# Block sums of the feed-forward weights by adding transfers instead of GpSimd, other shares for VectorE, and a few steps in another order

## The chip, the core and the metric

The kernel runs on one core of a Trainium2 chip, as one launch. The metric is the device time of a launch in microseconds (us). The engines are TensorE (PE; PEld is its weight load), VectorE (DVE), ScalarE (ACT), GpSimd (POOL) and SyncE (SP, which here only issues transfers). A smaller number is better.

## What is computed

One step of a two-layer network over 640 tokens (512 latent ones, 128 of context) of width 1024. Each layer is a feed-forward half, a token mixer and a second feed-forward half. Each of the six is modulated by a shift, a scale and a gate, which are a matrix product of a conditioning vector, and is followed by a residual and a LayerNorm:

```python
def _ffn_half(x, mod, slot, w1, w3, w2, g, b):
    h = _modulate(x, mod[:, 3 * slot], mod[:, 3 * slot + 1])
    f = (jax.nn.silu(h @ w1) * (h @ w3)) @ w2
    return _residual_post_norm(x, f, mod[:, 3 * slot + 2], FFN_RES, g, b)
# mod = (silu(cond) @ w_mod + b_mod).reshape(9, 1024), once for the latent and once for the context tokens
# x <- LN(alpha * x + weight * gate * f)
```

All is fp32. The inner width of a feed-forward half is 2816, that is 22 blocks of 128 columns (j = 0 to 21).

## The kernel before

**Precision.** TensorE multiplies in a reduced form, so each operand is split into a high part (ScalarE copies it, L299, tiles `wh`) and a low part (the difference, L306, tiles `wl`), and each product is made of three matmuls (high x high, high x low, low x high).

**Columns of a feed-forward half.** The blocks j = 0, 1, 2 are multiplied in the plain way. Blocks 3 to 21 are `Pair`s (19 in each half, 76 in all): W1 and W3 of a block are taken together as a 2 x 2 matrix of blocks a11, a12, a21, a22 (each 128 x 512 in memory, 256 KB), the activations as another (b11 and so on, and combinations of them, tiles `ta`, `tb`, made once for each half), and the product is made of 7 block products instead of 8. For that the weights have to be combined: s1 = a21 + a22, s2 = s1 - a11, s3 = a11 - a21, s4 = a12 - s2. The 7 products are of 12 matmuls of 320 columns each, 84 in a pair. `Pair.run` gives their order; its small closures (`u3`, `c12`, `gate1`, ...) put the results together on VectorE and ScalarE and are called one product later, by `slot`.

**Chunks.** The 22 blocks go in chunks of 4 (one of them a pair), 3, 3, 4, 4 and 4. After each chunk come the 8 blocks of W2 (tiles `o`), whose results are added to x (`resid`, L610).

**Weights.** `Stream` loads and converts all weights in the order of their use. `load` issues a load from SP into one of two buffers of 512 KB. `get` converts as far ahead as six slots of `wh` and `wl` allow, so five blocks ahead of the one that TensorE takes. `combine` makes s1 to s4 of a pair on GpSimd (L259, four instructions) into four buffers `ws` of 256 KB. The low parts of s2 and s4 (`ON_POOL`) are made on GpSimd as well, the five others on VectorE.

**Modulation units.** A unit is 128 columns of the modulation, with 512 KB of weights; there are 144. The first 24 are made by TensorE at the beginning. The 120 others are shared out in `vecq` order: some on VectorE inside feed-forward halves (`vec_mods`: per unit 4 multiplications with a sum, L460, and one small step, L463, paced by a credit at each call of `mods`, three in a pair and one for each block of W2), 16 in each of the first three halves; the rest inside the two mixers on TensorE (`mod_beside`: 16 small matmuls, L397, and a step of two, L415), 40 in layer 0 and 32 in layer 1.

**Mixer and norm.** The mixer's order is a table written out by hand (`SCHEDULES`), the same in both kernels. `rows_norm` ends each of the six parts: it adds the last blocks to x, takes the statistics and makes the next modulated input; `coef` makes the norm coefficients of the next part (tiles `gam`, `bet`) from the modulation.

## Time and profile before

| | us |
|---|---|
| median of 3 runs | 2677.38 (2677.23 to 2682.13) |
| the profiled execution | 2677.22 |
| its span, first to last instruction | 2675.0 |
| TensorE busy | 2537.6 (95%) |
| VectorE busy | 2068.8 (77%) |
| GpSimd busy | 1243.9 (46%) |
| ScalarE busy | 1176.7 (44%) |

A share of the span is an average over parts with different limits. Matmuls overlap one another, so a busy TensorE can still be one that waits a little before each group; for that the same work is compared in several places.

### The profile page before, as it was taken

To read this page: it belongs to the slowest core of one execution; us is meant where nothing else is said; L and a number is where in the kernel's file an instruction comes from. 1 tells how busy PE (TensorE), PEld (TensorE's weight loads), DVE (VectorE), ACT (ScalarE), POOL (GpSimd) and SP (SyncE) were. 2 spreads that over 40 slices of the span, in tenths; PEclk is the share of its full clock that TensorE was granted. 3 is DMA by queue.
4 is the path that set the end of the run, shared out by engine and by line. 5 is a ranking of instruction groups with operands and counts; after the bars stand their busy time and mean duration, and the time that the engine had idled before them with its cause. 6 is when DMAs were issued, how large, how long until landed. Compare 5 with 4: busy or idle time off the path is not lost. (4 is left out here: it accounts for less than half of the span.)

```text
span 2675.0 us, 49819 instructions
## 1 busy us (share of the span) xinstructions
PE 2537.6 (95%) x18662; PEld 2437.0 (91%) x18662; DVE 2068.8 (77%) x3759; ACT 1176.7 (44%) x2596; POOL 1243.9 (46%) x973
## 2 busy tenths in 40 slices
PE   7999999899999999999989999998998999999997
PEld 6999999889778999999989999998996798999997
DVE  6589899856764879988987998898586558777776
ACT  5233333555574533333453333334555735334333
POOL 1345445522444555544565454454234456435554
PEclk9999999999999999999999999998999999999998
DMA  7333332355344233333223333323452331222222
GB/s 266 120 94 107 100 103 91 106 165 148 96 125 156 72 99 99 102 109 104 71 82 99 100 103 109 105 87 125 141 159 80 104 123 44 78 85 84 83 79 72
DMA packets 130544, 285.88 MB, mean 107 GB/s; under 512 B 16832, under 2 KB 34560, under 8 KB 129664
## 3 DMA queue, kind: packets, MB, share of 16 engines
q1 hardware_dynamic: 110720, 247.04, 29.3%
q10 hardware_dynamic: 19584, 35.66, 4.2%
q8 instruction: 148, 2.42, 0.4%
q14 instruction: 92, 0.75, 0.1%
HBM read 254.95 MB, written 8.81 MB: 99 GB/s over the span
## 5 line engine op out<-in xcount | busy, mean ns | idle before, releaser
L306 DVE TENSOR_TENSOR wl<-wr,wh 128x512 fp32r<-128x512 f32 (+1 forms) x524 | 510.0, 987 | 74.2 <-ACT wh L299 73.1
L299 ACT CAST wh<-wr 128x512 fp32r<-128x512 f32 (+1 forms) x570 | 332.7, 607 | 484.5 <-DMA wr<-in_w 309.2
L485 PE MATMUL o<-gh,wh 128*128 128x256 f32 (+1 forms) x1408 | 439.7, 312 | 19.7 <-ACT gh L886 12.1
L485 PE MATMUL o<-gl,wh 128*128 128x256 f32 (+1 forms) x1408 | 438.6, 312 | 1.8
L485 PE MATMUL o<-gh,wl 128*128 128x256 f32 (+1 forms) x1408 | 436.4, 310 | 0.0
L847 PE MATMUL p<-hh,wh 128*128 128x320 f32 x1216 | 377.1, 310 | 10.9 <-DVE pm L858 10.8
L847 PE MATMUL p<-hl,wh 128*128 128x320 f32 x1216 | 377.2, 310 | 6.6 <-DVE hl L1010 6.6
L847 PE MATMUL p<-hh,wl 128*128 128x320 f32 x1216 | 377.4, 310 | 0.7 <-DVE wl L306 0.7
L259 POOL TENSOR_TENSOR ws<-wr 128x512 f32<-128x512 f32 x76 | 110.4, 1453 | 544.8 <-DMA wr<-in_w 508.5
L299 ACT CAST wh<-ws 128x512 fp32r<-128x512 f32 x304 | 185.7, 621 | 355.1 <-PE p L847 128.4
L306 POOL TENSOR_TENSOR wl<-ws,wh 128x512 fp32r<-128x512 f32 x152 | 239.9, 1582 | 189.2 <-ACT wh L299 188.6
L610 DVE SCALAR_TENSOR_TENSOR x<-o,gat,x 128x128 f32<-128x128 f32 (+2 forms) x404 | 193.0, 525 | 137.1 <-PE o L485 135.5
L485 PEld LDWEIGHTS o<-gh,wh 128*128 128x128 f32 x1408 | 267.7, 190 | 23.4 <-ACT gh L886 15.0
L485 PEld LDWEIGHTS o<-gl,wh 128*128 128x128 f32 x1408 | 267.9, 190 | 6.8 <-DVE gl L891 4.8
L485 PEld LDWEIGHTS o<-gh,wl 128*128 128x128 f32 x1408 | 267.5, 190 | 0.0
L847 PEld LDWEIGHTS p<-hh,wh 128*128 128x128 f32 x1216 | 228.9, 188 | 13.2 <-issue 12.2
L847 PEld LDWEIGHTS p<-hl,wh 128*128 128x128 f32 x1216 | 229.1, 188 | 7.7 <-DVE hl L1010 7.7
L847 PEld LDWEIGHTS p<-hh,wl 128*128 128x128 f32 x1216 | 229.2, 189 | 1.8 <-DVE wl L306 1.5
L460 DVE SCALAR_TENSOR_TENSOR scr<-wv,cb 128x512 f32<-128x512 f32 x192 | 174.8, 910 | 0.0
L259 POOL TENSOR_TENSOR ws<-wr,wr 128x512 f32<-128x512 f32 x76 | 130.4, 1715 | 0.6 <-DVE wl L306 0.6
L259 POOL TENSOR_TENSOR ws<-wr,ws 128x512 f32<-128x512 f32 x76 | 130.4, 1716 | 0.0
L306 DVE TENSOR_TENSOR wl<-ws,wh 128x512 fp32r<-128x512 f32 x152 | 129.2, 863 | 0.0
(434 smaller groups left out, 6604.3 us busy)
## 6 DMA issues: line engine op xcount, KB each, us to landing
wr<-in_w SPq DMA_DIRECT2D x176, 512.0 KB, 4.2
wm<-in_wmod ACTq DMA_DIRECT2D x136, 256.0 KB, 3.1
wr<-in_w SPq DMA_DIRECT2D x128, 256.0 KB, 2.7
wv<-in_wmt SPq DMA_DIRECT2D x96, 256.0 KB, 4.1
wm<-in_wmod SPq DMA_DIRECT2D x56, 256.0 KB, 5.3
wr<-in_w SPq DMA_DIRECT2D x64, 192.0 KB, 2.4
wr<-in_wint SPq DMA_DIRECT2D x24, 512.0 KB, 4.3
wr<-in_wo SPq DMA_DIRECT2D x16, 512.0 KB, 3.8
```

Source lines behind the costliest of these rows:

```text
L259: G.tensor_tensor(out=o, in0=x0, in1=x1, op=op)
L299: S.copy(hl[0], src[:, c0:c1])
L306: eng.tensor_tensor(out=t2, in0=src, in1=t.bitcast(F32), op=ALU.subtract)
L460: V.scalar_tensor_tensor(out=scr, in0=w[2 * i + hf], scalar=1.0, in1=cb[:, 2 * st + hf, :], op0=ALU.mult, op1=ALU.mult, accum_out=a[:, 2 * ...
L485: PE.matmul(out[:, :cn], whl[a][:, k, :], b[:, c0:c0 + cn], start=k == 0 and i == 0, stop=k == n - 1 and i == 2)
L610: V.scalar_tensor_tensor(out=c, in0=src, scalar=gat[:, d, s:s + 1], in1=c, op0=ALU.mult, op1=ALU.add)
L847: PE.matmul(out[:, :HN], w[a][:, k, :], b[k][c], start=k == 0 and i == 0, stop=k == 3 and i == 2)
```

## The change

1. **Sums by transfers.** `combine` is gone. `begin` makes one sum: a plain load from SP of one block into a `ws` buffer, and then one or two transfers from GpSimd's queue that add (`accum_op`) another block from HBM, or the finished s1, into the same buffer: s3 = a21 + a11, s1 = a21 + a22, s2 = a11 + s1, s4 = a12 + a11 + s1. The signs differ from before, and the steps that put the products together (`c12`, `quarters`) subtract where they added. A pair so takes 4 plain loads and 5 adding transfers of 256 KB, and of W3 only a22 is still loaded in the ordinary way (256 KB in place of 512 KB).
2. **One pair ahead.** The sums of the first pair of a half are begun when its a11 is converted; every other sum is begun for the next pair when the sum in its buffer has been converted.
3. **Order in a pair.** a11, a12, a22, s3, s1, s2, s4 instead of a11, a12, a22, s2, s3, s1, s4, and the five steps on the quarters stand together behind s2's product.
4. **Low parts.** Those of s2 and s4 go to VectorE (`ON_POOL` is empty).
5. **Units.** 28, 24 and 28 on VectorE in the first three halves instead of 16 each, and 20 in each mixer instead of 40 and 32.
6. **Norm.** `coef` stands ahead of the rows in `rows_norm`, and one `item` ahead of `res_half(1, 1)`.

```diff
-BLOCKS = ("a11", "a12", "a22", "s2", "s3", "s1", "s4")
+BLOCKS = ("a11", "a12", "a22", "s3", "s1", "s2", "s4")
...
             def pair(self, a, b):
                 r = len(self.src)
-                self.src += [(a, (KD, P)), (b, (KD, P))]
+                self.src += [(a, (KD, P)), (b[:, 4:8, :], (4, P))]
+                self.parts[r] = a[:, 0:4, :], a[:, 4:8, :], b[:, 0:4, :], b[:, 4:8, :]
...
+            def begin(self, nm, r):
+                d11, d12, d21, d22 = self.parts[r]
+                o = ppt.tile([P, 512], F32, tag="pt", name=f"ws{uid()}")
+                first = dict(s3=d21, s1=d21, s2=d11, s4=d12)[nm]
+                nc.sync.dma_start(out=o.rearrange("p (a b) -> p a b", b=P), in_=first)
+                for y in dict(s3=(d11,), s1=(d22,), s2=("s1",), s4=(d11, "s1"))[nm]:
+                    if isinstance(y, str):
+                        G.dma_start(out=o, in_=self.sums[r, y], accum_op=ALU.add)
+                    else:
+                        G.dma_start(out=o.rearrange("p (a b) -> p a b", b=P), in_=y, accum_op=ALU.add)
+                self.sums[r, nm] = o
...
+                            if (r, "s3") not in self.sums:
+                                for nm in BLOCKS[3:]:
+                                    self.begin(nm, r)
                         else:
-                            if r != self.blocks["pair"]:
-                                self.combine(r)
-                            src = self.blocks[shape]
+                            src = self.sums[r, shape]
+                            if r in self.after:
+                                self.done.append((shape, self.after[r], len(self.w)))
...
+                while self.done and self.done[0][2] < len(self.w):
+                    self.begin(*self.done.pop(0)[:2])
...
-        ON_POOL = ("s2", "s4")
+        ON_POOL = ()
...
             def c12(self, p3):
-                self.op(self.sl[:, HI], self.m[:, LO], p3, ALU.add)
+                V.tensor_tensor(out=self.sl[:, HI], in0=p3[:, :HN], in1=self.m[:, LO], op=ALU.subtract)
...
-            h, first = ffn(l, 0, h, first, 0 if l else KD, 2 * KD, lambda a, n, b: rows_norm(a, n, l, 0, (l, 1), b),
+            h, first = ffn(l, 0, h, first, 0 if l else KD, (28, 28)[l], lambda a, n, b: rows_norm(a, n, l, 0, (l, 1), b),
...
-            modq += [vecq.pop(0) for _ in range((4 if l else 5) * KD)]
+            modq += [vecq.pop(0) for _ in range((20, 20)[l])]
...
-            h, first = ffn(l, 1, h, first, 0, 0 if l else 2 * KD, lambda a, n, b: rows_norm(a, n, l, 2, nxt, b),
+            h, first = ffn(l, 1, h, first, 0, (24, 0)[l], lambda a, n, b: rows_norm(a, n, l, 2, nxt, b),
```

How the instructions stand on their engines is shown at one pair, j = 9, the last of the third chunk in the first half of layer 0. The names are those of the code with a number; behind "waits" stand the semaphores that a row waits for: DMAHW is the landing of a transfer issued from SP, DMASW of one issued from GpSimd, and DVE, PE, Activation and Pool are the engines.

GpSimd's queue before, all of it for this pair: the four sums, then the low parts of s2 and s4.

```order
L259 TENSOR_TENSOR ws_2605<-wr_2460 128x512 [waits DMAHW2_49,Pool_49]
L259 TENSOR_TENSOR ws_2606<-ws_2605,wr_2458 128x512 [waits DMAHW1_49,DVE_49,Pool_49]
L259 TENSOR_TENSOR ws_2607<-wr_2458,wr_2460 128x512 [waits DVE_49]
L259 TENSOR_TENSOR ws_2608<-wr_2458,ws_2606 128x512 [waits Pool_49]
L306 TENSOR_TENSOR wl_2618<-ws_2606,wh_2617 128x512 [waits PE_49,Activation_49]
L306 TENSOR_TENSOR wl_2680<-ws_2608,wh_2679 128x512 [waits PE_49,Activation_49]
```

GpSimd's queue now, for the same pair: s3, s1, s2, and twice s4 (ws_2575 is s1).

```order
L262 DMA ws_2545<-in_w 128x512 [waits DMAHW2_49,DMASW1_49,DVE_49]
L262 DMA ws_2575<-in_w 128x512 [waits DMASW5_49,DMAHW3_49,DMASW3_49,DVE_49]
L260 DMA ws_2596<-ws_2575 128x512 [waits DMAHW4_49,DMASW7_49,DVE_49]
L262 DMA ws_2621<-in_w 128x512 [waits DMAHW6_49,DVE_49]
L260 DMA ws_2621<-ws_2575 128x512 [waits DMASW1_49]
```

No computing instruction is left there; in their place stand transfers, of which the third waits for the landing of the second and the fifth for that of the fourth.

SP's queue before, around the loads of this pair (wr_2458 and wr_2460; `wv` are weights of units):

```order
L243 DMA wr_2296<-in_w 128x1024 [waits DMAHW4_49,DVE_49]
L448 DMA wv_2324<-in_wmt 128x512
L448 DMA wv_2428<-in_wmt 128x512 [waits DVE_49]
L243 DMA wr_2458<-in_w 128x1024 [waits DMAHW1_49,DMAHW5_49,DVE_49,Pool_49]
L243 DMA wr_2460<-in_w 128x1024 [waits DMAHW6_49,DVE_49]
```

SP's queue now, around the loads of this pair (wr_2518, wr_2520 and the four ws):

```order
L244 DMA wr_2518<-in_w 128x1024 [waits DMAHW7_49,DVE_49]
L244 DMA wr_2520<-in_w 128x512 [waits DMAHW0_49,DVE_49]
L456 DMA wv_2539<-in_wmt 128x512 [waits DMAHW1_49]
L257 DMA ws_2545<-in_w 128x512 [waits DMAHW2_49,DMASW1_49,DVE_49]
L257 DMA ws_2575<-in_w 128x512 [waits DMASW5_49,DMASW3_49,DMAHW3_49,DMASW2_49,DVE_49]
L257 DMA ws_2596<-in_w 128x512 [waits DMAHW4_49,DVE_49]
L456 DMA wv_2616<-in_wmt 128x512 [waits DMAHW5_49]
L257 DMA ws_2621<-in_w 128x512 [waits DMAHW6_49,DMASW4_49,DVE_49]
```

The loads of the sums have come in; that of s1 (ws_2575) waits, among others, for the last adding transfer of the pair before it (DMASW5), which reads the s1 that lies in the buffer.

VectorE's queue before, at the end of pair 8: the steps on its quarters, with a step of a unit (`scr`) and a low part between them:

```order
L858 TENSOR_TENSOR pm_2501<-pm_2501,p_2561 128x320 [waits DVE_49,PE_49]
L306 TENSOR_TENSOR wl_2588<-wr_2460,wh_2587 128x512 [waits DMAHW2_49,Activation_49]
L858 TENSOR_TENSOR pm_2501<-pm_2501,p_2585 128x320 [waits DVE_49,PE_49]
L858 TENSOR_TENSOR gf_2633<-pm_2501,p_2541 128x320 [waits DVE_49,PE_49]
L460 SCALAR_TENSOR_TENSOR scr_1621,va_2581<-wv_2229,cb_808 128x512 [waits DMAHW3_49]
L858 TENSOR_TENSOR gf_2633<-gf_2633,sl_2559 128x320 [waits DVE_49]
L858 TENSOR_TENSOR gf_2633<-pm_2501,p_2541 128x320
L858 TENSOR_TENSOR pm_2501<-pm_2501,p_2541 128x320
```

VectorE's queue now, at the same place, with the low parts of pair 9's sums between the steps:

```order
L312 TENSOR_TENSOR wl_2687<-ws_2545,wh_2686 128x512 [waits DMASW6_49,PE_49,Activation_49]
L921 TENSOR_TENSOR pm_2569<-p_2680,pm_2569 128x320 [waits PE_49]
L866 TENSOR_TENSOR pm_2569<-pm_2569,p_2643 128x320 [waits DVE_49]
L866 TENSOR_TENSOR gf_2728<-pm_2569,p_2619 128x320 [waits DVE_49]
L866 TENSOR_TENSOR gf_2728<-pm_2569,p_2619 128x320
L866 TENSOR_TENSOR pm_2569<-pm_2569,p_2619 128x320
L312 TENSOR_TENSOR wl_2712<-ws_2575,wh_2711 128x512 [waits DMASW7_49,Activation_49]
L866 TENSOR_TENSOR gf_2728<-gf_2728,sl_2641 128x320 [waits DVE_49]
L881 TENSOR_TENSOR sl_2641<-p_2706,pm_2569 128x320 [waits DVE_49,PE_49]
L312 TENSOR_TENSOR wl_2742<-ws_2596,wh_2741 128x512 [waits DMAHW4_49,DMASW0_49,Activation_49]
```

The five steps on the quarters stand in a row, and the low parts that follow wait for adding transfers.

## Rows read from the trace of the kernel before

**Rows 1.** The page: its first line, and busy time of each engine.
```profile
span 2675.0 us, 49819 instructions
PE 2537.6 (95%) x18662; PEld 2437.0 (91%) x18662; DVE 2068.8 (77%) x3759; ACT 1176.7 (44%) x2596; POOL 1243.9 (46%) x973
```
**Rows 2.** Busy time by stretch: pairs and W2 of chunks 2 to 6, four halves.
```profile
core 0: us, PE busy (x) PEld busy (x) DVE busy (x) ACT busy (x) POOL busy (x), PEclk, DMA share, GB/s
136.30:469.00 332.70, 324.93 (x2187) 322.05 (x2186) 302.19 (x505) 122.94 (x230) 167.02 (x103) 0.99 0.31 99
988.00:1321.70 333.70, 324.56 (x2187) 320.58 (x2186) 302.60 (x505) 122.56 (x230) 166.96 (x103) 1.00 0.31 99
1456.50:1789.20 332.70, 324.36 (x2187) 320.46 (x2186) 301.01 (x505) 122.84 (x230) 165.90 (x103) 1.00 0.31 99
2302.00:2622.20 320.20, 320.20 (x2187) 320.20 (x2186) 239.12 (x373) 126.15 (x232) 156.02 (x103) 1.00 0.26 81
```
**Rows 3.** The chain that ended last, in the fourth half: start, us, what.
```profile
2418.17 49.27 PE p L847 x336
2467.45 28.11 PE o L485 x192
```
**Rows 4.** VectorE, first half of layer 0, in order of time: start, us, instruction.
```profile
341.28 3.08 DVE L306 TENSOR_TENSOR wl<-wr,wh 128x512 fp32r<-128x512 f32 x2
366.15 0.68 DVE L306 TENSOR_TENSOR wl<-ws,wh 128x512 fp32r<-128x512 f32 x1
366.75 0.47 DVE L858 TENSOR_TENSOR sl<-pm,p 128x320 f32<-128x320 f32 x1
367.15 1.38 DVE L306 TENSOR_TENSOR wl<-ws,wh 128x512 fp32r<-128x512 f32 x1
373.43 0.68 DVE L460 SCALAR_TENSOR_TENSOR scr<-wv,cb 128x512 f32<-128x512 f32 x1
374.04 0.68 DVE L306 TENSOR_TENSOR wl<-wr,wh 128x512 fp32r<-128x512 f32 x1
```
**Rows 5.** GpSimd in order of time, the same half.
```profile
342.18 1.63 POOL L259 TENSOR_TENSOR ws<-ws,wr 128x512 f32<-128x512 f32 x1
343.77 1.75 POOL L259 TENSOR_TENSOR ws<-wr,wr 128x512 f32<-128x512 f32 x1
```
**Rows 6.** VectorE's forms by line, whole span: ns min/median/max, first and last start.
```profile
L306 DVE TENSOR_TENSOR wl<-ws,wh x152: 676/684/1812, 95.1 to 2611.8; 128x512 fp32r<-128x512 f32 x152
L891 DVE TENSOR_TENSOR gl<-gf,gh x76: 491/818/1921, 109.8 to 2625.4; 128x640 fp32r<-128x640 f32 x52, 128x320 fp32r<-128x320 f32 x24
```
**Rows 7.** TensorE in order of time, around one unit in layer 0's mixer.
```profile
623.70 0.28 PE L415 MATMUL t<-const,ms 128*128 128x2 f32 x2
623.91 0.65 PE L397 MATMUL t<-wm,silc 128*32 128x128 f32 x16
624.49 0.94 PE L1368 MATMUL rq<-idn,crq 128*128 128x128 f32 x6
```
**Rows 8.** Busy time by stretch, columns as in rows 2: the two mixers.
```profile
535.90:845.00 309.10, 288.48 (x2732) 255.09 (x2731) 188.20 (x440) 178.70 (x534) 105.95 (x121) 0.99 0.45 133
1859.00:2158.50 299.50, 280.78 (x2583) 248.31 (x2581) 189.05 (x438) 173.99 (x517) 106.90 (x120) 0.99 0.41 121
```
**Rows 9.** Transfers by issuing line: count, KB each, median us from issue to landing.
```profile
wr<-in_w SPq DMA_DIRECT2D x176, 512.0 KB, 4.2
wr<-in_w SPq DMA_DIRECT2D x128, 256.0 KB, 2.7
wv<-in_wmt SPq DMA_DIRECT2D x96, 256.0 KB, 4.1
```
**Rows 10.** Busy time by stretch, columns as in rows 2: the loads at the beginning.
```profile
8.00:36.00 28.00, 22.19 (x213) 18.45 (x211) 15.46 (x45) 14.39 (x28) 0.56 (x1) 1.00 1.04 386
```
**Rows 11.** GpSimd and ScalarE in order of time, first pair of the fourth half.
```profile
2246.53 1.34 POOL L991 TENSOR_TENSOR ta<-hf 128x320 f32<-128x320 f32 x1
2258.94 0.81 ACT L1004 CAST hh<-ta 128x320 fp32r<-128x320 f32 x2
```

70 lines of the change are left out of this document (18 added, 52 removed).

## The prediction

> **What bounds the kernel now.** I read the busy times first [rows 1]: TensorE has 2537.6 of 2675.0 us, so a gain must shorten TensorE's own list or its waits. Then I read the same work in the four feed-forward halves [rows 2]: the pairs and the W2 blocks of chunks 2 to 6, x2187 matmul records in each. The fourth half, which has no modulation units on VectorE, takes 320.2 us with TensorE busy in all of it; in the chain that ended last its pairs follow one another at 49.27 us for four [rows 3], so 12.32 us for a pair and 1.76 for each of its 7 products, and W2 takes 28.11. The three halves with 16 units take 332.7, 333.7 and 332.7: 12.5 + 13.5 + 12.5 = 38.5 us more, and there VectorE is busy in 302 us instead of 239. So TensorE's arithmetic bounds the fourth half, and VectorE holds it up in the other three.
>
> Why VectorE is that full shows in its instructions in order of time. A low part of 128x512 that starts at 366.15 is followed at 366.75, so it occupies VectorE for 0.60 us, a step of 320 columns (366.75 to 367.15) for 0.40, and a multiplication of a unit (373.43 to 374.04) for 0.61 [rows 4]. But two low parts at 341.28 take 3.08 together, and beside them GpSimd runs its sums, from 342.18 on [rows 5]. The same form has a median of 684 ns and a maximum of 1812 [rows 6]. I take GpSimd's computing for the cause of the long ones.
>
> The mixers come last [rows 8]: 309.1 us with 40 units, 299.5 with 32; TensorE is busy in 288.5 and 280.8, so it is their main load, but 20.6 and 18.7 us are idle for other engines' sake.
>
> **The change, part by part.** The sum is made against the profiled execution, 2677.22 us (span 2675.0 and 2.2 around it), 0.2 below the median of the runs.
>
> (a) Units in the mixers: 20 + 20 instead of 40 + 32, 32 fewer. Around one unit TensorE goes from 623.70 to 624.49, 0.79 us [rows 7], so 32 x 0.79 = 25.3 us leave its list. Some of that time will be waited instead, since the mixer's chain also runs over ScalarE, VectorE and GpSimd. From below I take 0.3 us for a unit (10 us); from above the difference of the two mixers, 9.6 us for 8 units, 1.2 each (38 us), though their tables differ. I take 0.6, a little below TensorE's own price because of the idle 20 us: **-19**.
>
> (b) VectorE in the pairs. Without long forms a pair costs it 7 low parts x 0.60 = 4.2, 7 steps x 0.40 = 2.8, two products of the same size, 0.8, and a `gl` of 640 columns at its median, 0.8 [rows 4, 6]: 8.6 us of the 12.32. The two low parts that come from GpSimd are in that. The credit gives (4 x 28 + 4) / 95 = 1.22 steps at each of three calls in a pair, at 0.61 and a small share for the closing step some 0.65: 2.4 us. Together 11.0, 89% of a pair; with 24 units 10.6, 86%. Now, with 16 units, VectorE is busy in 302 of 333 us, 91%, though it has less to do. I expect 9 of the 12.8 us that a half loses to come back; from below 0, from above all 38.5. Three halves: **-27**.
>
> (c) The wait that the change brings. Let me follow a sum. s1 of the next pair may only be loaded when this pair's last adding transfer (s1 into s4) has read it; then the load lands, then a22 is added, then GpSimd may issue s2's, then s4's first one, whose landing the last one waits for. From one last adding transfer to the next there are thus one load and three adding transfers in a row, and one more issue: a loop. Queued behind a waiting one are, on GpSimd, the other sums and at a half's first two pairs `ta` and the scaling of x; on SP, behind the load of s1, the raw loads and the units' weights. Who waits for a late s4 is ScalarE's copy, VectorE's low part and what stands behind it, and then TensorE. How long may the loop be? The low part of s1 follows the quarters of the pair before, which can begin when s2's product ends, 1.76 us before the next pair's start; five steps take 2.0, the copy and the low part some 1.3, so the first loop of a chunk starts some 1.6 us after the start of a pair. s4 must have landed 1.4 us (its copy and low part) before its product, the seventh: 6 x 1.76 - 1.4 = 9.2 us after the pair's start. In a chunk of four pairs three loops lie between: 3 x 12.32 + 9.2 - 1.6 = 44.5, so 14.8 us a loop; in one of three pairs two loops, 2 x 12.32 + 7.6 = 32.2, so 16.1. Over W2 the loop rests.
>
> No adding transfer is in the trace. The load of 256 KB has a median of 2.7 us, of 4.1 for units' weights, which are queued behind others [rows 9]. For an adding transfer of 256 KB the lower end is 2.7 + 0.3 for its issue; if it must read its target too, it costs up to what 512 KB cost, 4.2, and if it is queued as the units' weights are, 4.1 - 2.7 = 1.4 more: 5.6. I take 3.8, the load's median, half of the 1.5 us between the two sizes and 0.4 for its issue, as the loads it resembles most are the lonely ones. Loop: 2.7 + 3 x 3.8 + 0.4 = 14.5, just below 14.8: hidden, but only just; I put down **+4** for single late ones. Ends: 2.7 + 9.0 + 0.4 = 12.1 (no cost), and 4.1 + 16.8 + 0.5 = 21.4 (three chunks of four at 19.7 and two of three at 10.6 are 80 us in each half).
>
> The Trainium skill (DMA: Bandwidth & Descriptors, the section on the anatomy of one DMA on the gpsimd path) fits a transfer from GpSimd's queue as 2.0 us and its bytes at 436 GB/s. By that an adding transfer would take an estimated 2.6 us, the loop 10.9, and the sum would be 4 us lower; no run here shows it yet.
>
> Bytes: a half's 18 pairs here take 4 loads and 5 adding transfers more and one load less, 8 x 0.262 x 18 = 38 MB in 333 us, 113 GB/s on top of 99, and 12 more units 19: 231 GB/s; with the targets read too 302. At the beginning the engines move 386 GB/s at full share [rows 10]. So bandwidth alone doesn't bound it, but a transfer will meet others.
>
> (d) A half's first pair has its five adding transfers on GpSimd ahead of the last `ta`. Now that group starts at 2246.53 and is first used at 2258.94 [rows 11], 12.4 us later, of which its three steps need 4. The block of transfers takes some 10 us from the first load's landing. Between -2 us a half (VectorE without long forms there) and +4: **+4** in all.
>
> (e) The bunch of five steps on the quarters holds p7's bank until two of them are done, 0.8 us after s2's product, and the bank is wanted two products (3.5 us) later: nothing, as long as VectorE is less than 2.7 us behind; behind that, a lag comes through in full. `coef` and the moved `item` are a few short steps off TensorE's path: nothing, at most 1 us for each of six norms either way.
>
> Sum: 2677.2 - 19 - 27 + 4 + 4 = 2639.2; **I forecast 2639 us.**
>
> **Rivals.**
> R1, slower: the loop of (c) takes the place of VectorE as the bound. With 3.4 for the load (between both medians) and 4.6 for an adding transfer (512 KB's 4.2 and 0.4) it is 3.4 + 13.8 + 0.5 = 17.7 us: 3 x 17.7 - 44.5 = 8.6 lost in a chunk of four, 2 x 17.7 - 32.2 = 3.2 in one of three, 32 us in a half, the fourth half too, which loses nothing now. VectorE's waits hide beneath. Three halves at +32 - 12.8, one at +32, the mixers' -19 and (d)'s +4: 2752. It decides from a loop of about 16.4 us, an adding transfer of about 4.3. For it speaks that I find only 0.3 us to spare; against it, that six slots let single sums be late.
> The Trainium skill (SBUF — State Buffer, the note on how DVE blocks DMA) has a rule for R1: a transfer issued from GpSimd waits for its descriptors while VectorE copies or scales in its two-port form, 3100 ns instead of 620 in its example. The rows of VectorE in the pairs are of other forms, so I leave the chance as it is.
>
> R2, no change: a loop of about 15.9 costs 9.5 us a half, which eats what VectorE gives back (three at -3.3, one at +9.5), and the mixers give only 8: 2677 - 0.4 - 8 + 4 = 2673.
>
> R3, slower: VectorE's long forms stay, because making transfers on GpSimd holds it up as computing did. Then 36 low parts x 0.60 and 12 units x 4 x 0.61 come on top of 302: 353 us in a stretch that has 333, twice +20, once +10, with (a) and (d) 2677.2 - 19 + 50 + 4 = 2712. Against it: the long ones stand beside computing on GpSimd.
> The Trainium skill (SBUF — State Buffer, who interferes with whom) says that a VectorE instruction with two SBUF inputs meets only a GpSimd instruction that reads SBUF, not one that merely writes; by that rule R3 falls out. The long forms here agree with its first half: 1.54 us each beside the sums, 0.60 alone.
>
> R4, more than forecast: 1.0 us for each unit (32) and 36 of (b)'s 38.5, with (c) and (d) free: 2609.
>
> **How the numbers follow.** The forecast, 2620 to 2662, has 0.55; R1 0.23, R2 0.06, R3 0.06, R4 0.10. The range reaches from 2606, just below R4, to 2716, which takes in R3 and the smaller third of R1 (loops up to about 17); that leaves out some 0.16 above and 0.04 below. A difference of 0.2% (5.4 us) is about what a measurement tells from none. Faster: 0.55 + 0.10 + a third of R2 = 0.67; same 0.06 (the rest of R2 and the edges); slower 0.27.
>
> **What will show it.** Right: the pair stretches of the first three halves at 322 to 326 us, the fourth still at 320; low parts on VectorE with a mean near 0.69 us; adding transfers that land within 4 us; mixers some 12 and 7 us shorter. Wrong: four pairs of the fourth half over 50 us, ScalarE's copies of `ws` waiting for transfers, GpSimd's queue never empty in a chunk (R1); low parts still of 1.7 us (R3); mixers as long as before with more idle on TensorE (a).

## The result and the profile after

The changed kernel takes 3051.98 us (median; 3043.2 to 3055.88), the kernel before beside it 2678.82. The ratio is 1.138, with a 95% interval of 1.136 to 1.140: 373 us slower. The direction is that of the rival R1 of the prediction, the size several times R1's 75 us.

The page of the changed kernel, first line and busy times (before: [rows 1]):

```profile
span 3053.3 us, 50052 instructions
PE 2661.7 (87%) x18086; PEld 2515.9 (82%) x18086; DVE 1942.5 (64%) x4197; ACT 1152.5 (38%) x2534; POOL 836.7 (27%) x897
```

No engine is fuller than before, apart from TensorE, which has 576 fewer matmul records and is busy 124 us longer. So time went into waiting. Where, the busy times by stretch tell; columns as in [rows 2], and the same pairs and W2 blocks with the same x2187 records, but from the changed kernel:

```profile
142.90:567.90 425.00, 357.03 (x2186) 344.81 (x2186) 275.94 (x637) 119.69 (x229) 73.22 (x85) 0.93 0.69 175
1083.40:1502.90 419.50, 356.90 (x2187) 343.65 (x2186) 265.52 (x603) 119.70 (x229) 73.25 (x85) 0.93 0.69 172
1647.40:2075.60 428.20, 358.30 (x2187) 345.20 (x2187) 276.75 (x638) 119.44 (x229) 73.23 (x85) 0.93 0.69 174
2589.20:2999.00 409.80, 352.17 (x2187) 338.56 (x2186) 209.60 (x401) 119.64 (x229) 73.25 (x85) 0.94 0.63 149
```

92.3, 85.8, 95.5 and 89.6 us more than before: 363 of the 378 us of span. Read from the first and last matmul of each part, the pairs of these chunks lost 288 us in the four halves and their W2 blocks 77, to the end of the last one. The fourth half, which has no units on VectorE and lost nothing before, loses as much as the others, so the units aren't the cause. From here on I take the fourth half as the place to look at, up to the end of its last W2 block: 435.7 us after, 344.2 before.

The other stretches account for the rest. The way from a half's first matmul to chunk 2 grew by 5 to 6 us each time (73.2 instead of 67.8 in the fourth half), 22 in all; the mixers, in the stretches of [rows 8], gave this:

```profile
638.70:932.50 293.80, 270.83 (x2354) 239.87 (x2352) 187.84 (x438) 171.28 (x493) 105.83 (x120) 0.98 0.35 102
2147.20:2438.40 291.20, 272.17 (x2368) 240.01 (x2366) 188.99 (x438) 169.19 (x493) 106.16 (x120) 0.99 0.36 103
```

15.3 and 8.3 us shorter; measured up to the next norm's matmuls, 12.2 and 6.3, as the output blocks behind them gave some back. Some 10 us more lie in the norms, nearly all behind the first two halves.

What the engines wait for in the fourth half, from the view of waits (engine, line, releaser: us in total, times, longest):

```profile
DVE wl L312 <- ACT wh L305: 160.0, 60, 6.7
POOL ws L260 <- DMA ws<-in_w: 111.4, 25, 6.7
...
ACT wh L305 <- DMA ws<-ws: 87.9, 20, 6.8
ACT wh L305 <- DMA ws<-in_w: 59.3, 13, 7.6
...
PE p L855 <- ACT pm L903: 33.2, 10, 4.6
```

ScalarE's conversions wait for the adding transfers (147 us of 436), VectorE waits for ScalarE. The last row is how this reaches TensorE. It names `pm`, the copy of a pair's first product (L903), but the product that waits is that of s4 itself, as the rows at the end of a chunk's last pair show (start, us, instruction, idle before and its releaser):

```profile
2795.89 0.62 ACT L305 CAST wh<-ws 128x512 fp32r<-128x512 f32 x1 [4.89 <-DMA ws<-ws]
...
2796.79 0.41 ACT L903 COPY pm<-p 128x320 f32<-128x320 f32 x1
...
2797.25 0.41 PE L855 MATMUL p<-hh,wh 128*128 128x320 f32 x1 [3.73 <-ACT pm L903]
```

Twelve matmuls go from 2797.25 to W2's first one at 2799.34: one product, the last of the pair, which is that of s4. It needs s4's parts, and it writes the bank (one of four, of which a pair takes five) that held the same pair's first product; the copy that empties this bank stands behind s4's conversion in ScalarE's queue. In all ten waits of this row the product begins 0.74 us after that conversion ends, so the copy makes at most 7.4 of the 33.2 us, and the rest is s4 being late. s4 is converted 1.4 us ahead of its product here; before, it was 8.7 us (product at 2465.52):

```profile
2456.82 0.62 ACT L299 CAST wh<-ws 128x512 fp32r<-128x512 f32 x1 [1.13 <-DVE sl L858]
```

The chain of waits in the fourth half (start, us, what) shows the loop itself, in two turns:

```profile
2755.61 4.13 DMA ws<-in_w
...
2760.31 6.57 DMA ws<-in_w
...
2767.42 0.84 POOL ws L260
2768.26 0.89 POOL ws L262
2769.15 3.78 issue
2772.94 3.45 DMA ws<-ws
...
2780.57 5.78 DMA ws<-in_w
...
2792.48 3.32 DMA ws<-ws
...
2798.67 3.91 DMA wr<-in_w
...
2804.05 2.69 DMA wr<-in_w
...
2807.45 0.37 ACT gh L485
```

At 2755.61 the load of s1 goes out, when the last adding transfer of the pair before has landed; it lands after 4.13 us, a22's addition after 6.57, then come two issues, the landing of s4's first addition (in "issue", 3.78) and its second (3.45). In the second turn the load of s1 goes out at 2776.47, again with the landing, and a22's addition at 2780.57. From one landing of s4 to the next are 2776.4 - 2755.5 = 20.9 and 2795.8 - 2776.4 = 19.4 us; a pair needs 12.3. The last rows are the beginning of W2: its raw loads, one behind the other, and behind their conversions the copy of the last pair's result, `gh`.

How long the transfers took (issuing line, count, KB, median us to landing; before: [rows 9]):

```profile
ws<-in_w SPq DMA_DIRECT2D x304, 256.0 KB, 4.2
ws<-in_w POOLq DMA_DIRECT2D x228, 256.0 KB, 4.8
...
ws<-ws POOLq DMA_DIRECT2D x152, 256.0 KB, 3.3
```

Finally TensorE's clock. A wait costs more than its length. Two stretches of the changed kernel, a wait of TensorE and what follows (columns as in [rows 2]):

```profile
2773.80:2777.80 4.00, 0.17 (x2) 0.00 (x0) 0.66 (x2) 1.31 (x4) 0.88 (x1) 1.00 0.81 133
2777.90:2781.50 3.60, 3.60 (x15) 3.60 (x16) 3.60 (x7) 2.96 (x6) 0.84 (x1) 0.56 0.76 243
```

After 4 us with hardly a matmul the granted clock is 0.56 in the next 3.6 us, mostly the lower level of 1.2 GHz: 15 matmuls, where 24 fit at the pace before (12.32 us for 84). Over the whole half TensorE's same matmuls are busy 377.8 us instead of 344.2, at a mean granted clock of 0.95 instead of 1.00. Of the 91 us lost, 58 are thus idle time and 34 slower work behind it; 0.95 as a mean of 1.00 and one half means about 44 us at the lower level, which is about 22 us of those 34. What the other 12 are is open.

### The profile page after: what moved, and what is told of

It reads as the page before. It is cut to its first block, busy times and chain, and to the rows that moved or that the text cites. A ratio compares the mean times of both kernels' runs of the same rounds, so it can differ in the third digit from the quotient of the medians.

```text
span 3053.3 us, 50052 instructions
## 1 busy us (share of the span) xinstructions
PE 2661.7 (87%) x18086; PEld 2515.9 (82%) x18086; DVE 1942.5 (64%) x4197; ACT 1152.5 (38%) x2534; POOL 836.7 (27%) x897
## 3 DMA queue, kind: packets, MB, share of 16 engines
q0 software_dynamic: 54720, 99.64, 19.7%
## 5 line engine op out<-in xcount | busy, mean ns | idle before, releaser
L855 PE MATMUL p<-hh,wh 128*128 128x320 f32 x1216 | 411.0, 338 | 186.0 <-ACT pm L903 154.4
L305 ACT CAST wh<-wr 128x512 fp32r<-128x512 f32 (+1 forms) x570 | 330.2, 606 | 499.1 <-DMA wr<-in_w 365.5
L312 DVE TENSOR_TENSOR wl<-ws,wh 128x512 fp32r<-128x512 f32 x304 | 206.9, 689 | 475.4 <-ACT wh L305 475.2
L312 DVE TENSOR_TENSOR wl<-wr,wh 128x512 fp32r<-128x512 f32 (+1 forms) x524 | 382.2, 744 | 148.4 <-ACT wh L305 147.8
L262 POOL DMA_DIRECT2D ws<-in_w x228 | 235.5, 1037 | 813.8 <-DVE wl L312 451.1
L855 PE MATMUL p<-hl,wh 128*128 128x320 f32 x1216 | 402.6, 331 | 2.3 <-DVE hl L987 2.3
L855 PE MATMUL p<-hh,wl 128*128 128x320 f32 x1216 | 402.1, 331 | 0.0
L260 POOL DMA_DIRECT2D ws<-ws x152 | 129.6, 853 | 736.1 <-DMA ws<-in_w 540.1
L468 DVE SCALAR_TENSOR_TENSOR scr<-wv,cb 128x512 f32<-128x512 f32 x320 | 218.9, 684 | 1.1
L855 PE MATMUL p<-tq,wh 128*128 128x320 f32 x456 | 117.6, 312 | 0.0
L855 PE MATMUL p<-tc,wh 128*128 128x320 f32 x304 | 95.2, 313 | 0.0
```

Of the source, the lines that this page charges most:

```text
L260: G.dma_start(out=o, in_=self.sums[r, y], accum_op=ALU.add)
L262: G.dma_start(out=o.rearrange("p (a b) -> p a b", b=P), in_=y, accum_op=ALU.add)
L305: S.copy(hl[0], src[:, c0:c1])
L312: eng.tensor_tensor(out=t2, in0=src, in1=t.bitcast(F32), op=ALU.subtract)
L468: V.scalar_tensor_tensor(out=scr, in0=w[2 * i + hf], scalar=1.0, in1=cb[:, 2 * st + hf, :], op0=ALU.mult, op1=ALU.mult, accum_out=a[:, 2 * ...
L855: PE.matmul(out[:, :HN], w[a][:, k, :], b[k][c], start=k == 0 and i == 0, stop=k == 3 and i == 2)
```

## The experiments

Seventeen kernels; those told without an interval ran once, and I use them for differences of tens of us or for their stretches. For each the fourth half is the first thing to read, since TensorE alone bounds it in the kernel before. The table has the stretches from chunk 2 to the last W2 block, summed over the five chunks and read from the first and last matmul record of each (neighbours overlap by 0.2 us); us is the time of the kernel. Kernels whose fourth halves hold the same instructions show the scatter: 435.7 (changed) and 431.2 (e14), 359.2 (e9) and 355.1 (e10), 355.4 (e16) and 352.2 (e17), with up to 5 us in W2's sums. Less than some 5 us says nothing there.

| kernel | us | fourth half | its pairs | its W2 |
|---|---|---|---|---|
| before | 2678 | 344.2 | 222.4 | 123.3 |
| changed | 3052 | 435.7 | 292.0 | 145.4 |
| e1 eight buffers | 3028 | 406.5 | 257.3 | 150.7 |
| e2 s1 before a11 in s4 | 3016 | 434.7 | 285.3 | 150.9 |
| e3 plain transfers | 2819 | 379.0 | 230.4 | 150.0 |
| e4 sums on GpSimd | 2713 | 344.2 | 222.5 | 123.2 |
| e5 eight, all at once | 2980 | 365.5 | 225.1 | 141.6 |
| e6 half the width | 2876 | 388.7 | 241.9 | 148.3 |
| e7 s4 from s2 | 2889 | 398.9 | 245.6 | 154.7 |
| e8 hybrid | 2749 | 367.8 | 229.7 | 139.4 |
| e9 hybrid, later | 2719 | 359.2 | 229.8 | 131.0 |
| e10 as e9, units as changed | 2714 | 355.1 | 228.0 | 128.5 |
| e11 changed, later | 3109 | 442.9 | 292.3 | 152.1 |
| e12 as e4, units as before | 2682 | 344.2 | 222.5 | 123.1 |
| e13 as e5, later | 2984 | 365.6 | 223.1 | 144.0 |
| e14 units as before | 3069 | 431.2 | 292.4 | 140.4 |
| e15 as e5, still later | 2975 | 357.0 | 225.1 | 133.5 |
| e16 hybrid, still later | 2711 | 355.4 | 230.1 | 127.0 |
| e17 as e16, units as changed | 2719 | 352.2 | 227.5 | 126.2 |

**Which part of the change costs the time: e4, e12, e14.** e4 takes the sums back to GpSimd and leaves all else changed.

```diff
+                for o, x0, x1 in ((s3, a21, a11), (s1, a21, a22), (s2, s1, a11), (s4, a12, s2)):
+                    G.tensor_tensor(out=o, in0=x0, in1=x1, op=ALU.add)
-                                for nm in BLOCKS[3:]:
-                                    self.begin(nm, r)
```

> The changed kernel with its sums computed on GpSimd as before (full loads of both blocks, four additions, with the new signs), and all else as changed: order of products, bunch, all low parts on VectorE, 28/24/28 and 20/20 units, norm coefficients. Theory L: no transfer stands behind another, so the fourth half, without units, is back at 320 to 324; the first three, where VectorE had 302 us of work in 333 and now gets 18 x 2 low parts (24 us) and 12, 8 and 12 units (31 or 21 us) more beside a computing GpSimd, lie at 350 to 370; mixers as in the changed kernel, 294 and 291: 2720 to 2765 us in all. Rival O: the fourth half stays above 340.

Measured: 2713.43 us, 1.0126 times before (1.0108 to 1.0144). The first and the fourth half of this kernel, columns as in [rows 2]:

```profile
135.00:514.80 379.80, 358.26 (x2353) 352.79 (x2351) 352.50 (x679) 133.21 (x249) 121.92 (x76) 0.97 0.34 112
2343.60:2687.80 344.20, 344.18 (x2353) 343.86 (x2352) 266.13 (x431) 134.11 (x245) 121.15 (x78) 1.00 0.24 77
```

The fourth half is back at 344.2 to the tenth, with the new order of products, the bunch of steps and all low parts on VectorE. So of the 373 us the transfers cost 339 and all the rest 35. In the first half VectorE is busy 352.5 us: there the units are what holds TensorE up. e12 is e4 with the units as before, 16 in each of the three halves and

```diff
-            modq += [vecq.pop(0) for _ in range((20, 20)[l])]
+            modq += [vecq.pop(0) for _ in range((40, 32)[l])]
```

> The kernel before with the changed order of products, the bunch of steps, all low parts on VectorE and the norm coefficients ahead, but sums on GpSimd and units as before: the run with sums on GpSimd (2713 us) minus the shift of units. It prices the shift. If VectorE is full in the halves (gains of 18 us in the mixers, against 18, 6 and 22 us lost in the halves and 12 at their ends), this is 2675 to 2695 and the shift costs some 20 to 35; if the low parts on VectorE or the new order cost the time instead, it stays at 2715 to 2735.

Measured: 2682.03 us, 1.0014 (0.9998 to 1.0030). Parts 3, 4 and 6 of the change cost nothing that can be told from none, and the shift of units costs 31 us where the sums are on GpSimd. e14 makes the same shift back in the changed kernel:

> The changed kernel with the units as before, 16 on VectorE in each of the first three halves and 40 and 32 in the mixers. With sums on GpSimd the shift cost 31 us (2713 against 2682), since VectorE was full. Here VectorE is busy 64% of the span and waits for the sums: by theory Q the units fit into its waits, so undoing the shift only costs the mixers' 18.5 us: 3065 to 3080. If the units' loads (12, 8 and 12 MB halves of 512 KB each) and steps lengthen the loops, undoing the shift gives back more in the halves than the mixers lose: 3010 to 3045.

Measured: 3068.61 us, 17 more than with the shift. Where VectorE waits anyway the units fit into its waits, and the shift gains what the mixers give. With the units as before in both, e14 against e12, the transfers cost 387 us.

**Loop or bytes: e1, e2, e3, e6, e7.** e1 gives the fourth half eight buffers for sums; begun is each sum as before, when the one in its place has been converted.

```diff
+                if r > self.half4 and self.odd(r):
+                    o = pm.tile([P, 512], F32, tag="wm", name=f"ws{uid()}")
+                else:
                     o = ppt.tile([P, 512], F32, tag="pt", name=f"ws{uid()}")
```

> The changed kernel, but in the fourth half the sums of every second pair go into four more buffers (those of the units' weights, which rest there), so that no load of s1 has to wait until the last adding transfer of the pair before has read the old s1. Number, size and queue of the transfers stay. Theory L (a loop of latencies through the one buffer of s1, 19 to 21 us a turn against a pair of 12.3): the fourth half's chunks 2 to 6, 409.8 us now and 320.2 before, fall below 345, its four pairs from 66-69 to at most 54; the first three halves stay at 420 to 428. Rival B (the bytes: 2 KB packets of the adding queue take 178 ns instead of 84, so the 16 engines or the memory are the limit): the fourth half stays above 385, since all bytes are moved as before. Rival O (the new order of the products, the bunch of steps on the quarters and all low parts on VectorE): it stays at about 410.

Measured: 379.0 us in the stretch of the expectation (2592.2 to 2971.2), between its two bounds and held by neither, and four pairs at 63.6, 57.2 and 55.2; to the end of the last W2 block 406.5. The pairs gained 35 of their 70 us. e2 keeps the buffers and shortens the loop:

```diff
-                for y in dict(s3=(d11,), s1=(d22,), s2=("s1",), s4=(d11, "s1"))[nm]:
+                for y in dict(s3=(d11,), s1=(d22,), s2=("s1",), s4=("s1", d11))[nm]:
```

> The changed kernel, but s4 takes s1 first and a11 last, the same transfers in the other order. The last reader of s1 then ends one adding transfer from HBM sooner (its 4.8 us median and some 0.5 of issue): the loop goes from about 20 to 14.5 us. Theory L: per chunk of four pairs 3 loops, of three pairs 2, each 5 us shorter, so 15 and 10 us, 65 us in a half, 260 in all: about 2795 us, four pairs at 51 to 54. Rival B: the same bytes, so 3030 to 3060. Rival O: 3030 to 3060.

Measured: 3015.66 us, 36 less, nearly all from the first three halves; the fourth is unchanged at 434.7. The loop through s1's buffer, as the only cause, fell here. In e2's trace the turns are still 18.4 and 18.3 us, from the conversion of one s4 (2723.96) to the next (2742.32, 2760.60), but by another way:

```profile
2723.96 0.63 ACT wh L305
...
2725.33 3.33 DMA ws<-in_w
...
2730.09 5.93 issue
...
2736.04 6.18 DMA ws<-in_w
...
2742.32 0.63 ACT wh L305
```

s4 has one buffer too. It is converted, its load goes out and lands (3.3), s1 is added (issued at 2729.23, landed after 6.5, here in "issue"), then a11 (6.2), with the conversion and the issues 18.4. The medians to landing rose as well, to 6.0 and 4.7; I put that down to the two transfers that wait for s1 now going out within 2.2 us of each other, which no run shows. So there are several loops of like length, and one shortened leaves the others.

e3 and e6 price the transfers. e3 overwrites instead of adding, e6 adds half the columns.

```diff
-                        G.dma_start(out=o, in_=self.sums[r, y], accum_op=ALU.add)
+                        G.dma_start(out=o, in_=self.sums[r, y], accum_op=ALU.bypass)
```

> The changed kernel with the adding transfers turned into plain ones (they overwrite their target instead of adding to it, so the sums are missing from the result): same queue, same waits, same order. It prices the adding itself. If reading the target makes the transfer slow (rival B, and my own upper end of the forecast), packets on GpSimd's queue fall from 178 to about 85 ns and the time to landing from 4.8 to about 3 us, the loop from 20 to 15: some 2800 us. Theory L with the price in the queue of GpSimd (making descriptors, two hops through semaphores) and not in the adding: landing 4 us or more, loop at least 17.5, over 2920.

```diff
-                        G.dma_start(out=o, in_=self.sums[r, y], accum_op=ALU.add)
+                        G.dma_start(out=o[:, :256], in_=self.sums[r, y][:, :256], accum_op=ALU.add)
```

> The changed kernel, each adding transfer only 256 of its 512 columns wide (so half of every sum is missing from the result): same count, order, queue and waits, half the bytes that are added. Engine time in a pair falls from 11.8 to about 8.3 us, what it was where the transfers overwrote (2819 us). Rival B: 2790 to 2850 us. Theory Q: the landing is mostly fixed; if it falls by 0.5 us only (4.8 to 4.3, 3.3 to 2.9), the chain of load and three transfers is 1.5 us shorter and the time stays over 2950.

Measured: 2818.67 and 2875.65 us. The queue of the adding transfers in the changed kernel (packets, MB, share of 16 engines' span), then in e3, and e3's issues:

```profile
q0 software_dynamic: 54720, 99.64, 19.7%
```

```profile
q0 software_dynamic: 30400, 99.64, 10.4%
...
ws<-in_w POOLq DMA_DIRECT2D x228, 256.0 KB, 3.8
...
ws<-ws POOLq DMA_DIRECT2D x152, 256.0 KB, 2.3
```

Adding doubles the engines' time for the same 99.64 MB: 2 KB packets at a median of 178 ns, where a plain 2 KB packet takes 84 and e3's 4 KB packets 166. In landing times adding costs 1.0 us each, and half the width saves 0.8 and 0.6 (4.0 and 2.7). A chain of two such transfers from HBM and one from SBUF gets 3.0 and 2.2 us shorter, and its load 0.4 and 0.5, with less traffic beside it. For e3 theory L had asked for more than 2920 and was wrong by 100 us, while rival B's 2800 was missed by 19; for e6 Q was wrong by 75 and B by 25. Both runs shorten latency and bytes at once, so they price the adding and don't tell the theories apart.

e7 makes s4 of a12 and s2, with one adding transfer instead of two:

```diff
-                for y in dict(s3=(d11,), s1=(d22,), s2=("s1",), s4=(d11, "s1"))[nm]:
+                for y in dict(s3=(d11,), s1=(d22,), s2=("s1",), s4=("s2",))[nm]:
```

> The changed kernel, but s4 = a12 + s2 by one adding transfer from SBUF instead of a12 + a11 + s1 by two: four adding transfers in a pair instead of five, one of the two long ones from HBM less, the right result. Theory Q: s1's loop 4.2 + 5.3 + 3.9 = 13.4 us, s4's own loop 4.2 + 3.9 + 1.3 = 9.4, GpSimd waits for the landings of s1 and s2, 5 + 3.3 and 2.2 of issue = 10.5: all near or below 12.3, so 2720 to 2800 us. Rival B: engine time 10.4 instead of 11.8 us, a gain of a fifth to a third of the loss: 2930 to 2980.

Measured: 2888.95 us, the best of the versions that make every sum whole by transfers, 163 us under the changed kernel; again between the theories.

**The run that decides: e5.** Eight buffers in the fourth half, all sums of the next pair begun together, and on GpSimd the three transfers that wait for no other ahead of the two that wait for s1:

```diff
+                        for k, y in (("s3", d21), ("s1", d21), ("s4", d12), ("s2", d11)):
+                            nc.sync.dma_start(out=v[k], in_=y)
+                        for k, y in (("s3", d11), ("s1", d22), ("s4", d11)):
+                            G.dma_start(out=v[k], in_=y, accum_op=ALU.add)
+                        for k in ("s2", "s4"):
+                            G.dma_start(out=o[k], in_=o["s1"], accum_op=ALU.add)
```

> As the run with eight buffers in the fourth half, but there all four sums of the next pair are begun at once, when this pair's s3 has been converted, and s4's a11 is added ahead of the two transfers that wait for s1: GpSimd's queue then stands still for one landing in a pair instead of two, and no buffer is waited for. Same number and size of transfers. Theory Q (latency: three loops at once, through s1's buffer, through s4's own buffer, and through GpSimd's queue, which waits in order for two landings of about 5 us and issues five times 0.55, 12.6 us in a pair): the fourth half's chunks 2 to 6, from the second chunk's first pair to the end of the last W2 block 435.7 now, 406.5 with eight buffers, 344.2 before, fall below 365. Rival B (time of the 16 DMA engines: 896 packets of 2 KB at 84 ns and 640 at 178 ns are 11.8 us a pair of 12.3): four pairs stay at 55 or more, the half above 390.

Measured: 365.5 us, and the pairs at 37.1, 37.1, 52.1, 49.4 and 49.4, so at TensorE's own pace but for 3 us in one chunk. The fourth half of before, of the changed kernel and of e5, then one chunk's pairs of e5, columns as in [rows 2]:

```profile
2302.00:2646.20 344.20, 344.16 (x2353) 343.83 (x2351) 252.64 (x396) 133.91 (x245) 171.27 (x113) 1.00 0.25 77
```

```profile
2589.20:3024.90 435.70, 377.75 (x2353) 362.84 (x2351) 226.36 (x431) 128.92 (x245) 88.44 (x95) 0.95 0.60 143
```

```profile
2584.60:2950.10 365.50, 354.03 (x2353) 348.65 (x2351) 226.66 (x431) 129.64 (x245) 88.08 (x95) 0.98 0.71 169
...
2646.00:2683.00 37.00, 37.00 (x254) 37.00 (x254) 22.03 (x42) 14.41 (x28) 11.19 (x13) 1.00 0.89 196
```

e5 moves the same bytes with the same loads and adding transfers in less time, at a DMA share of 0.71 instead of 0.60, and its pairs run at full pace at 0.82 to 0.89. So neither the bytes nor the engines' time bound the pairs of the changed kernel, in the fourth half, the only one that was run so. What bounded them is latency in queues and buffers: four buffers, filled by up to three transfers in a row, and a GpSimd queue that waits in order for two landings in each pair. e1, against e5, shows that buffers without the other order were worth half of that.

**W2: e11, e13, e15.** With the pairs settled, e5 still loses 18 us in W2. I looked for it in the transfers that meet W2's raw loads, first in the changed kernel, by beginning a next chunk's sums behind the third W2 block:

```diff
+                            if j == j0:
+                                ws.wait[r0] = 3
```

> The changed kernel, with the sums of a chunk's first pair begun behind the third W2 block of the chunk before instead of within its last pair. Theory W: the W2 blocks of the fourth half, 145.4 us, fall to 133 or less, in the other halves likewise, at the price of up to 5 us in a chunk's first pair: 2960 to 3010 us. If W2 is slow because s4 comes late and so the look-ahead is empty when W2 begins, whatever the transfers then do, W2 stays over 140 and the time over 3030.

Measured: 3108.68 us, 57 slower, and W2 at 152.1. In the changed kernel this place gained nothing. In e5's fourth half the same delay:

> As the run in which the fourth half has eight buffers and begins all sums at once (365.5 us, pairs 37.1, 37.1, 52.1, 49.4, 49.4, W2 24.7, 28.1, 34.1, 30.6, 24.1), but in that half the sums of a chunk's first pair are begun behind the third W2 block of the chunk before instead of in its last pair. Theory W (where sums come early, W2 loses only because its raw loads meet the sums' transfers): W2 falls from 141.6 us in all to 130 or less (123.3 before), pairs stay within 2 us, the half at 345 to 354: the same bytes as in the changed kernel, at nearly the speed of the kernel before. If W2 is slow for another reason, or the first pair of a chunk gets its sums too late, the half stays at 362 or above. The other halves as in the changed kernel.

Measured: 365.6 us, W2 144.0, nothing gained. But its trace shows why; SyncE's, ScalarE's and TensorE's rows in one W2 block, in order of time (start, us, instruction, idle before and its releaser):

```profile
2765.12 1.82 SPq L264 DMA_DIRECT2D ws<-in_w  x4
2768.23 1.24 SPq L247 DMA_DIRECT2D wr<-in_w  x2
...
2774.30 0.62 ACT L322 CAST wh<-wr 128x512 fp32r<-128x512 f32 x1 [5.90 <-DMA wr<-in_w]
2774.83 0.45 ACT L502 CAST gh<-gf 128x320 fp32r<-128x320 f32 x1
...
2775.33 0.45 PE L510 MATMUL o<-gh,wh 128*128 128x256 f32 x1 [3.90 <-ACT gh L502]
```

The four loads of the sums go out at 2765.12, just ahead of two raw loads of W2, of which the first lands only at 2774.2, after 6.0 us. ScalarE waits for it 5.9 us, and behind that stands the copy of the last pair's result, for which TensorE waits 3.9. "Behind the third block" meant the very beginning of W2, as the look-ahead is five blocks, so e11 hadn't taken the transfers out of W2's way either. e15 puts it behind the sixth:

> As the eight-buffer run with all sums at once, but the sums of a chunk's first pair are begun behind the sixth W2 block of the chunk before, so that their loads go out when the last pair's result has long been copied. Theory W: W2 of chunks 2 to 6 in the fourth half 123 to 131 us (144 with the third block, 141.6 in the last pair, 123.3 before), pairs 37.1 and 49.4 to 51, the half 346 to 356, with all bytes and all adding transfers of the changed kernel. If W2's loss has another cause, the half stays over 362.

Measured: 357.0 us, W2 133.5: 1 and 2.5 us over what I expected, and 8 of e5's 18 us back, in one run each, where the scatter is up to 5. The place of the sums' transfers is thus likely a part of W2's loss where the sums are early; the hybrids below show it more firmly. The other 10 us, and the 22 in the changed kernel itself, are not settled. A chunk's last s4 is converted 10.5 us ahead of its W2 before, 3.4 to 4.7 us in the changed kernel, and 3.2 to 4.0 in e3, whose pairs are close to their pace and whose W2 still loses 27 us. So W2 begins there with its look-ahead spent, and in the chain above it waits for raw loads that go out only when the conversion of the late s4 has let them pass. That fits an emptied look-ahead, but no run took that away alone.

**A version between the two: e8, e9, e10, e16, e17.** If latency is the trouble, sums with enough lead should be free. The hybrid makes s3 and s1 by a load and one adding transfer a pair ahead, and s2 and s4 on GpSimd:

```diff
+                G.tensor_tensor(out=s2, in0=self.raw[r][:, :512], in1=self.sums[r, "s1"], op=ALU.add)
+                G.tensor_tensor(out=s4, in0=self.raw[r][:, 512:], in1=s2, op=ALU.add)
```

> s3 and s1 by one load and one adding transfer each, a pair ahead as changed; s2 = a11 + s1 and s4 = a12 + s2 on GpSimd as before; the units as before (16, 16, 16 on VectorE; 40 and 32 in the mixers), the rest as changed. Two adding transfers in a pair, each with about 12 us from the moment its buffer is free to its conversion, against 4.2 + 5.3 needed, none behind another; engine time some 6 us a pair. Theory Q and B both: the fourth half back at 344 to 348; the first three, with two computing instructions on GpSimd in a pair instead of six beside VectorE, at 350 to 360 (before 362 to 364): 2640 to 2670 us. If sums by transfers are late even so, the fourth half is over 360 and the whole over 2720.

Measured: 2749.18 us, 1.0262 (1.0236 to 1.0288), the fourth half at 367.8. The pairs were nearly at their pace (37.1, 37.8, 51.0, 50.6, 53.2), W2 wasn't (139.4). e9 begins a next chunk's sums behind the fourth W2 block:

> The hybrid (s3 and s1 by one load and one adding transfer a pair ahead, s2 and s4 on GpSimd, units as before), but the sums of a chunk's first pair are begun behind the fourth W2 block of the chunk before instead of within its last pair; everything else, bytes too, as in the hybrid. Theory W: W2 loses because its third and fourth raw load meet those sums' transfers (5.1 us to landing instead of 2.3 in the kernel before), and ScalarE, in order, has the copy of the last pair's result behind the conversion that waits for them, so TensorE waits 2.8 us. Then the five W2 blocks of the fourth half, 139.4 us in the hybrid, 123.3 before, fall to 130 or less, and the W2 block of its first chunk from 35.6 to 31 or less: 2680 to 2715 us. If W2 is slow for another reason (raw tiles of 256 KB, the new order of conversions), they stay over 136 and the whole over 2735.

Measured: 2719.27 us, 1.0152 (1.0133 to 1.0172), W2 131.0; the W2 block of the fourth half's first chunk stayed at 34.5. For that GpSimd's and VectorE's rows of e9 give the reason:

```profile
2297.59 0.86 POOL L263 DMA_DIRECT2D ws<-in_w  x1 [0.68 <-DMA ws<-in_w]
2298.18 7.05 POOL L822 TENSOR_SCALAR x<-x,deriv 128x640 f32<-128x640 f32 x8
...
2299.38 6.39 DVE L321 TENSOR_TENSOR wl<-wr,wh 128x512 fp32r<-128x512 f32 x1 [1.13 <-ACT wh L314]
```

GpSimd's eight instructions that scale x stand behind an adding transfer, and so run in W2. One low part that takes 0.69 us elsewhere takes 6.39 beside them, and W2's additions to x wait behind it. e16 begins the sums behind the sixth block, and so behind the scaling; e10 and e17 are e9 and e16 with the changed kernel's units.

> The same with the units as in the changed kernel: 28, 24 and 28 on VectorE, 20 in each mixer. The mixers and their ends give back about 18 us, as in the run with sums on GpSimd. With two computing instructions on GpSimd in a pair, VectorE's forms should be long less often: if VectorE then has room, the first three halves lose under 6 us each against the run without the shift and the total is 2665 to 2700; if VectorE is full at 28 units whatever GpSimd does, 10 to 20 us each and 2695 to 2750.

> The hybrid (two adding transfers in a pair, s2 and s4 on GpSimd, units as before) with the sums of a chunk's first pair begun behind the sixth W2 block. In the first chunk they now also stand behind the scaling of x on GpSimd, which had waited behind them until W2's residual additions met it (there a low part on VectorE took 6.4 us and W2 34.5 instead of 28.2). Theory W: W2 of the first chunk 28 to 30, W2 of chunks 2 to 6 125 to 130, the fourth half at 346 to 350, the first three at 348 to 356 (before 362 to 364): 2640 to 2670 us. Otherwise 2700 and more.

> The same with units 28, 24, 28 on VectorE and 20 in each mixer. With the fourth block this was no dearer than the units as before (2714 against 2719). The mixers give back 18.5 us; the first three halves lose 3 to 10 each: 2635 to 2670 us, from 12 below to 8 above the run with the units as before.

Measured: e10 2713.67 us, 1.0128 (1.0099 to 1.0156); e16 2711.17, 1.0126 (1.0109 to 1.0143); e17 2719.13, 1.0153 (1.0128 to 1.0179). In e16 the first chunk's W2 block is back at 28.3 and W2 at 127.0, as expected, but the fourth half is at 355.4 instead of 346 to 350, and the first three are at 363.0, 369.3 and 368.3, where I had 348 to 356 (before, to the same point, 362.1, 363.6 and 361.8). None of these beats the kernel before. In e8, e9 and e16 a chunk's last s4 is converted 6.9 to 9.7 us ahead of its W2 alike, and the fourth half's W2 takes 139.4, 131.0 and 127.0: in the hybrid it is mostly the place of the sums' transfers that costs in W2. In e16 VectorE is busy only 280 to 283 us in those halves, some 45 less than before, and still they are 8 to 14 us slower than its fourth half; what holds them is open. The shift of units moved the hybrid by less than the runs scatter.

## Why the prediction was wrong

**(c) is the step that failed, in its sizes and in what it left out.** The loop was there, link by link as described, and R1's signs were in the trace: four pairs at 66 to 68 us, and ScalarE's conversions of `ws` waiting for transfers. I took 2.7 us for the load: it is 4.2. I took 3.8 with the issue for an adding transfer: in the median 4.8 from HBM (6.57 and 5.78 for a22's in the two turns shown) and 3.3 from SBUF, and 0.5 more from a landing to the next issue. That made 14.5, and 19.4 to 20.9 were measured, near the upper bound of 21.4. Here the choice failed: I went by the loads that ran alone ("the loads it resembles most are the lonely ones"), while I had written that each half would get 38 MB more and that "a transfer will meet others".

With the measured loop my own formula does well: 3 x 20 - 44.5 = 15.5 for four pairs, 2 x 20 - 32.2 = 7.8 for three, 62 us in a half; the pairs lost 69.6. So for the pairs the mis-sized term was the loop, and with 20 us in it R1 would have come out near 195 us slower. The rest of the 373 is in what follows, and in the 38 us that R1 took off for VectorE's relief, of which nothing showed.

What was left out: s4's own buffer is a second loop (18.3 us in e2), and GpSimd's queue a third, an estimated 12.6 us from two landings of about 5 us and five issues of 0.55 in each pair; it wasn't measured alone. e2 shortened one loop and gained nothing in the fourth half.

**"Over W2 the loop rests"** was the second failure. W2 lost 22 us in the fourth half (145.4 instead of 123.3), which no term held.

**"Against it, that six slots let single sums be late"** was wrong as an argument. Not single sums were late, but one in every pair, and a lead that isn't made up again is soon spent: 1.4 us for s4 instead of 8.7. The path from there was the one that (c) names, over ScalarE's copy to TensorE, which waited 33 us in front of s4's products in the fourth half. What had no term is that the stops cost TensorE its clock, about 22 us more in that half.

**Bytes.** I estimated 302 of 386 GB/s and said that bandwidth alone wouldn't bound it. By packets it is tighter: 896 packets of 2 KB at 84 ns and 640 at 178 are 11.8 us of the 16 engines for a pair of 12.3. The verdict still held, as e5's pairs ran at full pace with all of them, at a share of up to 0.89.

**(a)** was right: -19 forecast, 23.6 us less in the mixers' stretches, 18.5 up to the next norm.

**(b)** had the right cause for the long forms and the wrong worth. The low parts from `ws` are short in the changed kernel:

```profile
L312 DVE TENSOR_TENSOR wl<-ws,wh 128x512 fp32r<-128x512 f32 x304 | 206.9, 689 | 475.4 <-ACT wh L305 475.2
```

689 ns as the mean of 304 instructions, near the median of [rows 6], and a unit's step has 684. So R3 is out. The Trainium skill (SBUF — State Buffer, who interferes with whom) says that a VectorE instruction with two SBUF inputs meets a GpSimd instruction only if that reads SBUF; the trace agrees, with 689 ns beside transfers and 6.39 us in e9 beside GpSimd's scaling of x. But the 27 us were not to be had by freeing VectorE alone: in e16 it has 45 us less to do in a half, and the halves are no faster than before.

**(d)** had the right place and too small a price: +4 for `ta`, and 22 measured in the four first chunks. In the fourth half 3.8 of its 5.4 us lie in the W2 block of that chunk. What came late there was the scaling of x, which I had named in (c) as queued behind the transfers and then not priced. In the changed kernel, fourth half:

```profile
2564.87 7.04 POOL L813 TENSOR_SCALAR x<-x,deriv 128x640 f32<-128x640 f32 x8
...
2568.04 4.42 DVE L312 TENSOR_TENSOR wl<-wr,wh 128x512 fp32r<-128x512 f32 x1
```

Before, the scaling ran under the first pair; now it runs in W2 (from 2557.3), and holds a low part for 4.42 us, 3.7 more than its usual 0.69. No run moved the scaling alone.

**(e)** was right in its sum: e12 has all of it, and its ratio to before is 1.0014, with an interval that holds 1. In part that is luck. In its profile the first three halves are 2.3 to 2.5 us shorter, and from their last W2 matmul to the next part's first it is 21.9, 20.4 and 20.4 us instead of 18.5, 18.5 and 22.1: changes of more than the 1 us for each norm that I had allowed.

**The Trainium skill's price for a transfer.** By the fit in the Trainium skill (DMA: Bandwidth & Descriptors, the anatomy of one DMA on the gpsimd path) a transfer of 256 KB takes an estimated 2.6 us. e3's plain transfers within SBUF come near it with 2.3; those from HBM took 3.8, and adding ones 3.3 and 4.8. The measurement decides: for adding transfers among others that fit is low by a fifth to nearly a half.

## What to carry to other kernels

A transfer that depends on another costs its full latency, some 4 to 6 us here with its issue, so count the links from one use of a buffer to the next, for every buffer and every queue that waits in order, with the durations of transfers that meet others; if any such loop is longer than the work it feeds, it becomes the pace, and shortening one of several gains little. Look-ahead that runs through an in-order engine is no reserve against an operand that is late every time: what stands behind it stops too (in e13 the copy of a finished result, for which TensorE waited 3.9 us), and TensorE's clock falls on top. Where a part moves to transfers, begin the independent ones first and with a buffer to spare, and look at what else uses the queues at that moment.
